# Gate/up of a SwiGLU block: Strassen products added onto read PSUM regions, the element-wise work on VectorE, weight splits in product order

## The chip, the cores and the metric

The kernel runs on one core of a Trainium2 chip. The metric is the time of one execution on the device in microseconds, as the median of several runs; less is better. TensorE does the matrix products, VectorE, ScalarE and GpSimd the element-wise work, and SyncE issues most of the transfers. SBUF is the memory on the core from which the engines work, and PSUM is the memory into which TensorE adds its products; a PSUM bank holds 512 fp32 numbers for each of 128 partitions.

## The reference

A hybrid decoder trunk of two layers on 512 tokens with 1024 channels, in fp32. Each layer is a mixer (layer 0: a forgetting attention beside a sparse attention; layer 1: trailing means over 2, 4, 8 and 16 positions) and then a SwiGLU block, both between RMS norms. The change concerns the first half of the SwiGLU blocks:

```python
DEPTH, SEQ, D_MODEL, FFN_HIDDEN = 2, 512, 1024, 2816
h = rmsnorm(x, g2)
act = silu(h @ w_gate) * (h @ w_up)      # "gate/up": (512, 1024) x (1024, 2816), twice
x = x + rmsnorm(act @ w_down, g3)        # "down"
```

## The kernel before

Every fp32 product is made of three fast ones: each operand is split into a high part (a copy rounded to the fast format, on ScalarE, L237) and a low part (the rest, a subtraction, L238), and `three` (L326 to L328) adds high x high, low x high and high x low in PSUM. Tiles named `wh` and `wl` are the parts of a weight block, `uh`/`ul` and `th`/`tl` those of the input.

The class `Ffn` computes gate/up. The 2816 columns are 22 chunks of 128, taken as 11 pairs. For a pair and one of the two weights (an *item*; gate and up alternate, 22 items a layer) the 256 columns by 1024 rows of the weight are a 2 x 2 matrix of blocks, a11, a12, a21, a22 (first index the column chunk, second the half of the rows), and so is the input (halves of rows, halves of the tokens). A Strassen-Winograd step makes the four 128 x 256 quadrants of the result from seven block products (named after their weight side: 11, 12, 22, s1, s2, s3, s4) instead of eight, each of 12 matmuls of 128x256. The s are sums of the a blocks, made by `comb` in place on the raw tiles (L906); the sums on the input's side come from `combine` (tiles `tt`, L873), once a layer. For the first three pairs of layer 0 and the first two of layer 1 (`self.ws`) two products with the first half of the tokens ran ahead in `front` while the norm of the second half was computed; their items have five products instead of seven. I call them *short*, the others *long*. `run` takes a long pair, a short pair, and so on, and then the long pairs that are left.

An item's two raw tiles (`wr`, 512 KB each) are loaded by SyncE (L894); the tag has four buffers, so the tiles of item i+2 take those of item i. The parts have ten buffers, five products' worth. `run` writes the splits of item i+1 (`pair_weights`), then the first products of item i (`begin`), the last of item i-1 (`end`, then `gate_done` or `up_done`), and the rest of item i (`middle`). Engines work in the order that the program is written in, apart from priorities; `comb` has a raised one. The products lie in three PSUM banks (psA, psS, psO), one half bank each; p5 and p7, p4 and p6 share a bank. VectorE adds them up in tiles `comb` by seven sums of 128x256 (L951 to L957 and L963, the last of an item). `next_engine` deals operations out in turn by a string: 'vg' means VectorE and GpSimd alternately. `sadd` (weight and input sums) is 'vg', `mul` (the gate-up product, L977) 'g', the low parts 'v'. After the last item, `down` multiplies the result by the third weight (L774 to L776).

Of the kernel before, what the change touches and what calls it, by code (L numbers as in the profile page):

```python
# [13 lines left out]
P = 128  # L14
# [39 lines left out]
    sadd='vg',  # L54
    mul='g',
# [57 lines left out]
def trunk(ctx: ExitStack, tc, x, norm_g, w_in, b_f, cmp_pe, cmp_w1, cmp_w2, w_out,  # L113
# [186 lines left out]
    def transpose_pair(dst, srcs, ks, tag, gcol=None):  # L300
        """dst(k) -> (hi, lo) of [128, 256]: the transposed column blocks ks of two token tiles"""
# [36 lines left out]
    # ================= layer 0: FoX || NSA =================  # L338
# [30 lines left out]
    # -- block compression --  # L369
# [63 lines left out]
    # -- keys and queries, stacked along the contraction --  # L433
# [49 lines left out]
    # -- values: [token, d] with high and low parts side by side --  # L483
# [36 lines left out]
    # -- forget gates and branch gates, projected beside the values of the NSA branches --  # L520
# [30 lines left out]
    # -- softmax and P^T for one (head, branch) and half of the queries --  # L551
# [215 lines left out]
    # -- out[token, :] = sum over contraction chunks; the last chunks token tile by token tile --  # L767
# [60 lines left out]
    class Ffn:  # L828
# [8 lines left out]
        def weights(self, p):  # L837
            """the first column chunk of a pair, whose two products with the first half of the tokens run ahead"""
            self.ws[p] = [load_w(cols(w_[self.layer], 2 * p * P, P), [P, KC, P], pair_g if p < CFG["eg"] else None)
                          for w_ in (w_gate, w_up)]  # L840
# [23 lines left out]
        def combine(self):  # L864
            """T1 = B12 - B11, T2 = B22 - T1, T3 = B22 - B12, T4 = B21 - T2, each transposed and split"""
# [23 lines left out]
        def pair_weights(self, w_, p):  # L889
            """the blocks of two column chunks and the sums of a Strassen-Winograd step, high and low parts"""  # L890
# [16 lines left out]

            if p not in self.ws:
                put("11", a11)
            put("22", a22)  # L910
            comb(a22, a21, a22, ALU.add)
            put("s1", a22)
            comb(a21, a11, a21, ALU.subtract)
            put("s3", a21)
            if p not in self.ws:
                put("12", a12)
            comb(a11, a22, a11, ALU.subtract)
            put("s2", a11)
            comb(a12, a12, a11, ALU.subtract)
            put("s4", a12)  # L920
            return W

        def run(self):
# [6 lines left out]
            def prod(o, w, b):  # L930
                for k in range(4):
                    three(o, w[0][k], w[1][k], b[0][k], b[1][k], k == 0, k == 3)

            def begin(W, p, i):
                m = {"pre": self.acts[2 * p + i] if p in self.ws else None, "W": W, "a": BANK("psA"), "b": BANK("psS"), "c": BANK("psO"), "x": XE([P, 4, 256], label="comb")}
                m["p1"], m["p5"], m["p7"], m["p4"], m["p6"] = (
                    m["a"][:, 0:256], m["b"][:, 0:256], m["b"][:, 256:512], m["c"][:, 0:256], m["c"][:, 256:512])
                if m["pre"] is None:
                    prod(m["p1"], W["11"], B11)
                    nc.scalar.activation(m["x"][:, 0, :], m["p1"], AF.Copy)  # L940
                prod(m["p4"], W["22"], T[4])
                return m

            def middle(m):
                W, x_ = m["W"], m["x"]
                prod(m["p5"], W["s1"], T[1])
                prod(m["p7"], W["s3"], T[3])
                if m["pre"] is None:
                    prod(m["p1"], W["12"], B21)
                prod(m["p6"], W["s2"], T[2])  # L950
                nc.vector.tensor_add(x_[:, 1, :], m["p6"], x_[:, 0, :] if m["pre"] is None else m["pre"][:, 256:])  # L951
                nc.vector.tensor_add(x_[:, 2, :], m["p7"], x_[:, 1, :])
                nc.vector.tensor_add(x_[:, 3, :], m["p5"], x_[:, 2, :])
                nc.vector.tensor_add(x_[:, 1, :], m["p5"], x_[:, 1, :])
                nc.vector.tensor_add(x_[:, 2, :], m["p4"], x_[:, 2, :])
                if m["pre"] is None:
                    nc.vector.tensor_add(x_[:, 0, :], m["p1"], x_[:, 0, :])  # L957

            def end(m, last):
                x_ = m["x"]  # L960
                p3 = BANK("psS")[:, 0:256] if last else m["p5"]
                prod(p3, m["W"]["s4"], B22)
                nc.vector.tensor_add(x_[:, 1, :], p3, x_[:, 1, :])  # L963

            def gate_done(m):
                x_ = m["x"] if m["pre"] is None else m["x"][:, 1:, :]
                nc.scalar.activation(x_, x_, AF.Silu)

            def up_done(p, g, m):
# [3 lines left out]
                for r in range(2):  # L973
                    r0 = 2 * r if r or m["pre"] is None else 1
                    a_ = self.acts[2 * p + r].rearrange("p (a b) -> p a b", a=2)[:, r0 - 2 * r:, :]
                    rows = slice(r0, 2 * r + 2)
                    next_engine("mul").tensor_tensor(a_, xg[:, rows, :], xu[:, rows, :], op=ALU.mult)  # L977

            def finish_(i):
                end(ms[i], i == len(todo) - 1)  # L980
# [5 lines left out]
            ws = [self.pair_weights(todo[0][1], todo[0][0])]  # L986
            ms = []
            for i in range(len(todo)):
                if i + 1 < len(todo):
                    ws.append(self.pair_weights(todo[i + 1][1], todo[i + 1][0]))  # L990
# [195 lines left out]
```

## Time and profile before

| quantity | value |
|---|---|
| time, median of 3 runs | 1079.62 us (1078.86 to 1079.63) |
| profiled execution, span | 1076.4 us |
| its gate/up, first combine sum to last item's end, layer 0 | 304.69 to 548.07 us |
| the same, layer 1 | 711.60 to 950.49 us |
| TensorE busy | 1032.2 us, 96% |
| VectorE busy | 783.5 us, 73% |
| ScalarE busy | 563.5 us, 52% |
| GpSimd busy | 511.0 us, 47% |

The profiled execution is told by its span, from the first to the last instruction; no time of its own outside the span is recorded, and the median of the runs is 3.2 us longer than it. Busy times of engines overlap. A share over the whole span is an average over stages with different limits, so the rows further down are mostly cut at the ends of items.

### The profile page before, as it was taken

To read this page: it belongs to the slowest core of one execution; us is meant where nothing else is said; L and a number is where in the kernel's file an instruction comes from. 1 tells how busy PE (TensorE), PEld (TensorE's weight loads), DVE (VectorE), ACT (ScalarE), POOL (GpSimd) and SP (SyncE) were. 2 spreads that over 40 slices of the span, in tenths; PEclk is the share of its full clock that TensorE was granted. 3 is DMA by queue.
4 is the path that set the end of the run, shared out by engine and by line. 5 is a ranking of instruction groups with operands and counts; after the bars stand their busy time and mean duration, and the time that the engine had idled before them with its cause. 6 is when DMAs were issued, how large, how long until landed. Compare 5 with 4: busy or idle time off the path is not lost.

```text
span 1076.4 us, 18708 instructions
## 1 busy us (share of the span) xinstructions
PE 1032.2 (96%) x6892; PEld 944.7 (88%) x6892; DVE 783.5 (73%) x1488; ACT 563.5 (52%) x1172; POOL 511.0 (47%) x421
## 2 busy tenths in 40 slices
PE   7999999999999999999999998989999999999997
PEld 6899888977899989899988886989889999988886
DVE  4449797767578999999991034788999999992123
ACT  5557797688465344444472234664444444472221
POOL 3815667666762444434454353362444334454340
PEclk9999999999999999999999999799999999999999
DMA  7920202233603333333334355003343343334222
GB/s 226 205 62 21 79 12 70 61 115 121 177 22 97 112 107 109 105 113 98 104 113 132 118 159 154 21 11 90 97 118 101 96 118 99 99 118 137 88 69 79
DMA packets 153419, 108.55 MB, mean 101 GB/s; under 512 B 11764, under 2 KB 134512, under 8 KB 153328
## 3 DMA queue, kind: packets, MB, share of 16 engines
q1 hardware_dynamic: 152528, 106.22, 33.7%
q8 instruction: 54, 0.88, 0.3%
q10 hardware_dynamic: 800, 1.15, 0.3%
q14 instruction: 37, 0.30, 0.1%
HBM read 101.88 MB, written 2.10 MB: 97 GB/s over the span
## 4 chain that ended last, share of the span: by engine, by line
PE 73%; DVE 15%; ACT 4%; issue 4%; DMA 2%; POOL 2%; DVEq 0%; POOLq 0%; ACTq 0%; SPq 0%
PE psA L328 5%; PE psA L326 5%; PE psA L327 5%; DVE wl L238 5%; PE psS L326 5%; PE psS L328 5%; PE psS L327 5%; PE psO L326 3%; PE psO L327 3%; PE psO L328 3%; PE psT L774 2%; PE psT L775 2%; PE psO L775 2%; PE psT L776 2%; PE psO L774 2%
## 5 line engine op out<-in xcount | busy, mean ns | idle before, releaser
L237 ACT ACTIVATE wh<-wr 128x512 fp32r<-128x512 f32 x420 | 252.8, 626 | 314.2 <-DVE wr L906 106.9
L238 DVE TENSOR_TENSOR wl<-wr,wh 128x512 fp32r<-128x512 f32 x318 | 297.0, 959 | 106.0 <-ACT wh L237 105.3
L238 POOL TENSOR_TENSOR wl<-wr,wh 128x512 fp32r<-128x512 f32 x102 | 144.4, 1426 | 137.7 <-ACT wh L237 128.6
L328 PE MATMUL psA<-uh,wl 128*128 128x256 f32 (+1 forms) x408 | 129.3, 317 | 0.5 <-DVE wl L238 0.5
L326 PE MATMUL psA<-uh,wh 128*128 128x256 f32 (+1 forms) x408 | 128.7, 315 | 0.4 <-ACT comb L940 0.4
L327 PE MATMUL psA<-ul,wh 128*128 128x256 f32 (+1 forms) x408 | 128.1, 314 | 0.0
L906 POOL TENSOR_TENSOR wr<-wr,wr 128x512 f32<-128x512 f32 x44 | 57.4, 1304 | 142.0 <-DVE wr L906 97.6
L906 POOL TENSOR_TENSOR wr<-wr 128x512 f32<-128x512 f32 x44 | 59.3, 1348 | 105.9 <-DVE wl L238 80.1
L326 PE MATMUL psS<-th,wh 128*128 128x256 f32 x352 | 100.9, 287 | 6.6 <-ACT wh L237 4.8
L328 PE MATMUL psS<-th,wl 128*128 128x256 f32 x352 | 101.4, 288 | 4.5 <-DVE wl L238 4.3
L327 PE MATMUL psS<-tl,wh 128*128 128x256 f32 x352 | 100.5, 286 | 0.0
L328 PE MATMUL psO<-th,wl 128*128 128x256 f32 x352 | 99.8, 284 | 0.6 <-DVE wl L238 0.6
L327 PE MATMUL psO<-tl,wh 128*128 128x256 f32 x352 | 99.8, 284 | 0.0
L326 PE MATMUL psO<-th,wh 128*128 128x256 f32 x352 | 99.5, 284 | 0.0
L328 PEld LDWEIGHTS psA<-uh,wl 128*128 128x128 f32 x408 | 78.3, 192 | 6.9 <-DVE wl L238 2.8
L326 PEld LDWEIGHTS psA<-uh,wh 128*128 128x128 f32 x408 | 78.2, 192 | 4.6 <-ACT comb L940 0.6
L327 PEld LDWEIGHTS psA<-ul,wh 128*128 128x128 f32 x408 | 78.3, 192 | 3.8
L977 POOL TENSOR_TENSOR act<-comb,comb 128x512 f32<-128x512 f32 (+1 forms) x44 | 71.9, 1649 | 11.6 <-DVE comb L963 6.2
L326 PEld LDWEIGHTS psS<-th,wh 128*128 128x128 f32 x352 | 67.7, 192 | 8.0 <-ACT wh L237 5.8
L328 PEld LDWEIGHTS psS<-th,wl 128*128 128x128 f32 x352 | 67.8, 193 | 6.8 <-DVE wl L238 6.7
L264 POOL TENSOR_SCALAR E<-E,ri 128x128 f32<-128x128 f32 (+3 forms) x48 | 54.6, 1139 | 40.0 <-DVE ri L582 16.7
L328 PEld LDWEIGHTS psO<-th,wl 128*128 128x128 f32 x352 | 67.4, 192 | 1.5 <-DVE wl L238 1.5
(343 smaller groups left out, 2972.2 us busy)
## 6 DMA issues: line engine op xcount, KB each, us to landing
wr<-in_ffn_w_gate_dram SPq DMA_DIRECT2D x49, 512.0 KB
wr<-in_ffn_w_up_dram SPq DMA_DIRECT2D x49, 512.0 KB
wr<-in_ffn_w_down_dram SPq DMA_DIRECT2D x44, 512.0 KB
wr<-in_attn_w_in_dram SPq DMA_DIRECT2D x20, 512.0 KB
wr<-in_attn_w_out_dram SPq DMA_DIRECT2D x8, 512.0 KB
x<-in_x_dram SPq DMA_DIRECT2D x4, 512.0 KB
gbc<-in_norm_g_dram SPq DMA_DIRECT2D x8, 256.0 KB
h<-in_x_dram SPq DMA_DIRECT2D x4, 512.0 KB
```

The lines of the kernel that those rows point to most:

```text
L237: nc.scalar.activation(hi, src, AF.Copy)
L238: next_engine(key).tensor_tensor(lo, src, r32(hi), op=ALU.subtract)
L264: (nc.vector if k == "v" else nc.gpsimd).tensor_scalar(e, e, s1, None, op0=ALU.mult)
L326: nc.tensor.matmul(psum, wh, ah, start=first, stop=False)
L327: nc.tensor.matmul(psum, wh, al, start=False, stop=False)
L328: nc.tensor.matmul(psum, wl, ah, start=False, stop=last)
L774: nc.tensor.matmul(o, acts[c][0][:, tok], wh[k], start=first, stop=False)
L775: nc.tensor.matmul(o, acts[c][0][:, tok], wl[k], start=False, stop=False)
L776: nc.tensor.matmul(o, acts[c][1][:, tok], wh[k], start=False, stop=last)
L906: next_engine("sadd").tensor_tensor(o, x0, x1, op=op)
L977: next_engine("mul").tensor_tensor(a_, xg[:, rows, :], xu[:, rows, :], op=ALU.mult)
```

## The change

GpSimd's part of gate/up goes to VectorE: `sadd` and `mul` become 'v'. Two products get no PSUM region of their own any more: 22 is added by TensorE onto the region of p7 after VectorE read that, and s4 onto p5. In long items 12 is added onto p1 likewise, after ScalarE read it. A fourth block tile, s3, replaces one of the sums in place. The seven sums of 128x256 in an item become three (L956 to L958) and one of 128x512 that adds one `comb` row to both halves of a bank (L966). The bank psO is not used in gate/up any more. Quadrant p1 is read from PSUM by the silu (L972) and by the product (L979) in long pairs. The gate-up product is L979 to L981, and the combinations stand in L907 (these are line numbers of the changed kernel). `pair_weights` becomes a generator that gives the splits in the order in which the products are done: 11 and s2 of item i+1, then 22 and s4 of item i, then s3, s1 and 12 of item i+1. The products go 11, s2 of an item, then 22, s4 of the item before, then s3, s1, 12.

```diff
-    sadd='vg',
-    mul='g',
+    sadd='v',
+    mul='v',
...
         def pair_weights(self, w_, p):
             raws = []
             for a in range(2):
                 raw = T([P, KC, P], "wr", CFG["wr"])
@@ -905,20 +906,23 @@
                 with tc.high_priority(CFG["hpw"]):
                     next_engine("sadd").tensor_tensor(o, x0, x1, op=op)
 
+            s3 = JK("s3").rearrange("p (k c) -> p k c", k=4)
             if p not in self.ws:
                 put("11", a11)
-            put("22", a22)
-            comb(a22, a21, a22, ALU.add)
-            put("s1", a22)
-            comb(a21, a11, a21, ALU.subtract)
-            put("s3", a21)
+            comb(s3, a11, a21, ALU.subtract)
+            comb(a21, a21, a22, ALU.add)
+            comb(a11, a21, a11, ALU.subtract)
+            put("s2", a11)
+            yield W
+            put("s3", s3)
+            put("s1", a21)
             if p not in self.ws:
                 put("12", a12)
-            comb(a11, a22, a11, ALU.subtract)
-            put("s2", a11)
             comb(a12, a12, a11, ALU.subtract)
+            yield W
+            put("22", a22)
             put("s4", a12)
-            return W
+            yield W
 
         def run(self):
             rest = [p for p in range(NF // 2) if p not in self.ws]
@@ -927,67 +931,72 @@
             B11, B21, B22 = self.block(0, 0), self.block(1, 0), self.block(1, 1)
             T = self.T
 
-            def prod(o, w, b):
+            def prod(o, w, b, start):
+
                 for k in range(4):
-                    three(o, w[0][k], w[1][k], b[0][k], b[1][k], k == 0, k == 3)
+                    wh, wl, bh, bl = w[0][k], w[1][k], b[0][k], b[1][k]
+                    nc.tensor.matmul(o, wh, bh, start=start and k == 0, stop=False, skip_group_check=True)
+                    nc.tensor.matmul(o, wh, bl, start=False, stop=False, skip_group_check=True)
+                    nc.tensor.matmul(o, wl, bh, start=False, stop=k == 3, skip_group_check=True)
 
             def begin(W, p, i):
-                m = {"pre": self.acts[2 * p + i] if p in self.ws else None, "W": W, "a": BANK("psA"), "b": BANK("psS"), "c": BANK("psO"), "x": XE([P, 4, 256], label="comb")}
-                m["p1"], m["p5"], m["p7"], m["p4"], m["p6"] = (
-                    m["a"][:, 0:256], m["b"][:, 0:256], m["b"][:, 256:512], m["c"][:, 0:256], m["c"][:, 256:512])
-                if m["pre"] is None:
-                    prod(m["p1"], W["11"], B11)
+                pre = self.acts[2 * p + i] if p in self.ws else None
+                m = {"pre": pre, "W": W, "a": BANK("psA"), "c": BANK("psS"), "x": XE([P, 4, 256], label="comb")}
+                m["p1"], m["p6"], m["p5"], m["p7"] = m["a"][:, 0:256], m["a"][:, 256:], m["c"][:, 0:256], m["c"][:, 256:]
+                if pre is None:
+                    prod(m["p1"], W["11"], B11, True)
                     nc.scalar.activation(m["x"][:, 0, :], m["p1"], AF.Copy)
-                prod(m["p4"], W["22"], T[4])
+                prod(m["p6"], W["s2"], T[2], pre is not None)
                 return m
 
             def middle(m):
                 W, x_ = m["W"], m["x"]
-                prod(m["p5"], W["s1"], T[1])
-                prod(m["p7"], W["s3"], T[3])
+                prod(m["p7"], W["s3"], T[3], True)
+                prod(m["p5"], W["s1"], T[1], False)
+                nc.vector.tensor_add(x_[:, 0, :], m["p6"], x_[:, 0, :] if m["pre"] is None else m["pre"][:, 256:])
+                nc.vector.tensor_add(x_[:, 3, :], m["p7"], x_[:, 0, :])
+                nc.vector.tensor_add(x_[:, 3, :], m["p5"], x_[:, 3, :])
                 if m["pre"] is None:
-                    prod(m["p1"], W["12"], B21)
-                prod(m["p6"], W["s2"], T[2])
-                nc.vector.tensor_add(x_[:, 1, :], m["p6"], x_[:, 0, :] if m["pre"] is None else m["pre"][:, 256:])
-                nc.vector.tensor_add(x_[:, 2, :], m["p7"], x_[:, 1, :])
-                nc.vector.tensor_add(x_[:, 3, :], m["p5"], x_[:, 2, :])
-                nc.vector.tensor_add(x_[:, 1, :], m["p5"], x_[:, 1, :])
-                nc.vector.tensor_add(x_[:, 2, :], m["p4"], x_[:, 2, :])
+                    prod(m["p1"], W["12"], B21, False)
+
+            def end(m):
+                x_ = m["x"]
+                prod(m["p7"], m["W"]["22"], T[4], False)
+                prod(m["p5"], m["W"]["s4"], B22, False)
+                nc.vector.tensor_tensor(x_[:, 1:3, :], m["c"].rearrange("p (a b) -> p a b", a=2),
+                                        x_[:, 0:1, :].to_broadcast([P, 2, 256]), op=ALU.add)
+
+            def gate_done(m):
+                x_ = m["x"]
                 if m["pre"] is None:
-                    nc.vector.tensor_add(x_[:, 0, :], m["p1"], x_[:, 0, :])
-
-            def end(m, last):
-                x_ = m["x"]
-                p3 = BANK("psS")[:, 0:256] if last else m["p5"]
-                prod(p3, m["W"]["s4"], B22)
-                nc.vector.tensor_add(x_[:, 1, :], p3, x_[:, 1, :])
-
-            def gate_done(m):
-                x_ = m["x"] if m["pre"] is None else m["x"][:, 1:, :]
-                nc.scalar.activation(x_, x_, AF.Silu)
+                    nc.scalar.activation(x_[:, 0, :], m["p1"], AF.Silu)
+                nc.scalar.activation(x_[:, 1:, :], x_[:, 1:, :], AF.Silu)
 
             def up_done(p, g, m):
                 xg, xu = g["x"], m["x"]
                 if m["pre"] is None:
                     self.acts[2 * p], self.acts[2 * p + 1] = RAW(2 * p), RAW(2 * p + 1)
-                for r in range(2):
-                    r0 = 2 * r if r or m["pre"] is None else 1
-                    a_ = self.acts[2 * p + r].rearrange("p (a b) -> p a b", a=2)[:, r0 - 2 * r:, :]
-                    rows = slice(r0, 2 * r + 2)
-                    next_engine("mul").tensor_tensor(a_, xg[:, rows, :], xu[:, rows, :], op=ALU.mult)
+                    nc.vector.tensor_mul(self.acts[2 * p][:, 0:256], m["p1"], xg[:, 0, :])
+                next_engine("mul").tensor_tensor(self.acts[2 * p][:, 256:], xg[:, 1, :], xu[:, 1, :], op=ALU.mult)
+                next_engine("mul").tensor_tensor(self.acts[2 * p + 1].rearrange("p (a b) -> p a b", a=2), xg[:, 2:, :], xu[:, 2:, :], op=ALU.mult)
 
             def finish_(i):
-                end(ms[i], i == len(todo) - 1)
+                end(ms[i])
                 if i % 2 == 0:
                     gate_done(ms[i])
                 else:
                     up_done(todo[i][0], ms[i - 1], ms[i])
 
-            ws = [self.pair_weights(todo[0][1], todo[0][0])]
+            gens = [self.pair_weights(w_, p) for p, w_ in todo]
+            ws = [next(gens[0])]
+            next(gens[0])
             ms = []
             for i in range(len(todo)):
                 if i + 1 < len(todo):
-                    ws.append(self.pair_weights(todo[i + 1][1], todo[i + 1][0]))
+                    ws.append(next(gens[i + 1]))
+                next(gens[i])
+                if i + 1 < len(todo):
+                    next(gens[i + 1])
                 ms.append(begin(ws[i], todo[i][0], i % 2))
                 if i:
                     finish_(i - 1)
```

Two places show what that does to the order on VectorE. `comb_9` to `comb_11` are the results of three successive items, 9 and 10 a long pair; `wl` are low parts, `wr` raw tiles (54 and 55 of item 9, 56 and 57 of item 10, 58 and 59 of item 11). At the border of items 9 and 10, VectorE had before:

```order
L238 TENSOR_TENSOR wl_112_5281<-wr_56_5276,wh_112_5280 128x512
L238 TENSOR_TENSOR wl_113_5285<-wr_57_5278,wh_113_5284 128x512
L951 TENSOR_TENSOR comb_9_5315<-psO_45_5314,comb_9_5315 128x256
L906 TENSOR_TENSOR wr_57_5278<-wr_57_5278 128x512
L952 TENSOR_TENSOR comb_9_5315<-psS_96_5313,comb_9_5315 128x256
L957 TENSOR_TENSOR comb_9_5315<-psA_38_5312,comb_9_5315 128x256
L953 TENSOR_TENSOR comb_9_5315<-psS_96_5313,comb_9_5315 128x256
L954 TENSOR_TENSOR comb_9_5315<-psS_96_5313,comb_9_5315 128x256
L238 TENSOR_TENSOR wl_114_5290<-wr_57_5278,wh_114_5289 128x512
L955 TENSOR_TENSOR comb_9_5315<-psO_45_5314,comb_9_5315 128x256
L906 TENSOR_TENSOR wr_56_5276<-wr_57_5278,wr_56_5276 128x512
L238 TENSOR_TENSOR wl_115_5295<-wr_57_5278,wh_115_5294 128x512
```

There it has now:

```order
L958 TENSOR_TENSOR comb_9_5280<-psS_96_5279,comb_9_5280 128x256
L238 TENSOR_TENSOR wl_111_5254<-wr_56_5241,wh_111_5253 128x512
L238 TENSOR_TENSOR wl_112_5258<-wr_55_5138,wh_112_5257 128x512
L238 TENSOR_TENSOR wl_113_5262<-wr_54_5136,wh_113_5261 128x512
L238 TENSOR_TENSOR wl_114_5266<-s3_10_5245,wh_114_5265 128x512
L956 TENSOR_TENSOR comb_10_5403<-psA_39_5401,comb_10_5403 128x256
L238 TENSOR_TENSOR wl_115_5270<-wr_57_5243,wh_115_5269 128x512
L238 TENSOR_TENSOR wl_116_5274<-wr_56_5241,wh_116_5273 128x512
L907 TENSOR_TENSOR wr_56_5241<-wr_56_5241 128x512
L966 TENSOR_TENSOR comb_9_5280<-psS_96_5279,comb_9_5280 128x512
L907 TENSOR_TENSOR s3_11_5376<-wr_58_5372,wr_59_5374 128x512
L907 TENSOR_TENSOR wr_59_5374<-wr_59_5374 128x512
```

Before, the low parts of item 10 (from `wr_56`, `wr_57`) began ahead of item 9's sums, and those of item 9 were all done. Now the low parts of 22 and s4 of item 9 (`wl_112` from `wr_55`, `wl_113` from `wr_54`, the last reads of these tiles) stand behind the low part of s2 of item 10 (`wl_111`), and s3 of item 11, the first read of `wr_58` and `wr_59`, stands seven rows further down.

The second place is the border between items 7 and 8, a short gate and a short up item (`wr_52` and `wr_53` are item 8's). Before, on VectorE:

```order
L238 TENSOR_TENSOR wl_99_4967<-wr_50_4942,wh_99_4966 128x512
L238 TENSOR_TENSOR wl_100_5072<-wr_53_5069,wh_100_5071 128x512
L906 TENSOR_TENSOR wr_53_5069<-wr_53_5069 128x512
L951 TENSOR_TENSOR comb_7_5098<-psO_43_5097,act_3_4078 128x256
L952 TENSOR_TENSOR comb_7_5098<-psS_94_5096,comb_7_5098 128x256
L238 TENSOR_TENSOR wl_101_5077<-wr_53_5069,wh_101_5076 128x512
L953 TENSOR_TENSOR comb_7_5098<-psS_94_5096,comb_7_5098 128x256
L954 TENSOR_TENSOR comb_7_5098<-psS_94_5096,comb_7_5098 128x256
L906 TENSOR_TENSOR wr_52_5067<-wr_53_5069,wr_52_5067 128x512
L955 TENSOR_TENSOR comb_7_5098<-psO_43_5097,comb_7_5098 128x256
L238 TENSOR_TENSOR wl_102_5082<-wr_53_5069,wh_102_5081 128x512
L238 TENSOR_TENSOR wl_103_5087<-wr_52_5067,wh_103_5086 128x512
```

And now:

```order
L980 TENSOR_TENSOR act_9_5104<-comb_5_4820,comb_6_4943 128x256
L981 TENSOR_TENSOR act_10_5105<-comb_5_4820,comb_6_4943 128x512
L907 TENSOR_TENSOR s3_8_5039<-wr_52_5035,wr_53_5037 128x512
L957 TENSOR_TENSOR comb_7_5066<-psS_94_5065,comb_7_5066 128x256
L907 TENSOR_TENSOR wr_53_5037<-wr_53_5037 128x512
L958 TENSOR_TENSOR comb_7_5066<-psS_94_5065,comb_7_5066 128x256
L907 TENSOR_TENSOR wr_52_5035<-wr_53_5037,wr_52_5035 128x512
L907 TENSOR_TENSOR wr_52_5035<-wr_52_5035 128x512
L238 TENSOR_TENSOR wl_98_5044<-wr_52_5035,wh_98_5043 128x512
L238 TENSOR_TENSOR wl_99_5048<-wr_51_4914,wh_99_5047 128x512
L238 TENSOR_TENSOR wl_100_5052<-wr_50_4912,wh_100_5051 128x512
L238 TENSOR_TENSOR wl_101_5056<-s3_8_5039,wh_101_5055 128x512
```

Before, the first low part of item 8 (`wl_100`, of 22) stood ahead of item 7's sums. Now the first one (`wl_98`, of s2) stands behind the sums of item 7 (L957, which reads p7, and L958, which reads p5) and behind four combinations of item 8's raw tiles.

## Rows read from the trace of the kernel before

**Rows 1.** The page: engine totals, and the granted clock in 40 slices.

```profile
PE 1032.2 (96%) x6892; PEld 944.7 (88%) x6892; DVE 783.5 (73%) x1488; ACT 563.5 (52%) x1172; POOL 511.0 (47%) x421
...
PEclk9999999999999999999999999799999999999999
```

**Rows 2.** Timeline of TensorE's matmuls, 440 to 482 us: start, duration, instruction.

```profile
445.06 0.28 PE L326 MATMUL psS<-uh,wh 128*128 128x256 f32 x1
...
445.90 0.28 PE L327 MATMUL psS<-ul,wh 128*128 128x256 f32 x1
```

**Rows 3.** Timeline of VectorE: the last sum of two items, same columns.

```profile
478.81 0.41 DVE L963 TENSOR_TENSOR comb<-psS,comb 128x256 f32<-128x256 f32 x1
...
540.72 0.41 DVE L963 TENSOR_TENSOR comb<-psS,comb 128x256 f32<-128x256 f32 x1
```

**Rows 4.** Windows between item ends: length; PE, PEld, DVE, ACT, POOL busy; clock; DMA; GB/s.

```profile
304.69:347.05 42.36, 40.64 (x339) 40.00 (x338) 36.59 (x58) 25.18 (x49) 20.98 (x17) 1.00 0.26 75
...
370.92:410.34 39.42, 37.30 (x291) 36.36 (x290) 36.71 (x59) 16.72 (x28) 16.79 (x12) 0.96 0.37 108
410.34:448.86 38.52, 36.36 (x291) 35.05 (x290) 36.79 (x60) 16.70 (x28) 16.79 (x12) 1.00 0.38 110
448.86:548.07 99.21, 98.08 (x800) 96.27 (x799) 94.36 (x156) 48.99 (x85) 42.80 (x31) 1.00 0.37 109
...
770.52:809.94 39.42, 37.31 (x291) 36.37 (x290) 36.70 (x60) 16.73 (x28) 16.78 (x12) 0.96 0.37 107
809.94:950.49 140.55, 139.42 (x1136) 136.85 (x1135) 134.80 (x220) 68.69 (x119) 60.88 (x43) 1.00 0.37 108
```

**Rows 5.** Timeline of VectorE inside one item, 454 to 459 us.

```profile
454.06 0.41 DVE L952 TENSOR_TENSOR comb<-psS,comb 128x256 f32<-128x256 f32 x1
454.39 0.41 DVE L957 TENSOR_TENSOR comb<-psA,comb 128x256 f32<-128x256 f32 x1
...
456.98 1.28 DVE L238 TENSOR_TENSOR wl<-wr,wh 128x512 fp32r<-128x512 f32 x2
458.18 0.42 DVE L963 TENSOR_TENSOR comb<-psS,comb 128x256 f32<-128x256 f32 x1
458.51 1.67 DVE L238 TENSOR_TENSOR wl<-wr,wh 128x512 fp32r<-128x512 f32 x1
```

**Rows 6.** Timeline of GpSimd at the same place.

```profile
458.34 1.30 POOL L906 TENSOR_TENSOR wr<-wr 128x512 f32<-128x512 f32 x1 [2.77 <-DVE wl L238]
```

**Rows 7.** Timeline of VectorE near 304 us, a 512-column operation on PSUM.

```profile
303.98 0.68 DVE L814 TENSOR_TENSOR mq<-psO,gbc 128x512 f32<-128x512 f32 x1
```

**Rows 8.** Timeline of SyncE's queue: issues of raw weight tiles.

```profile
361.20 1.90 SPq L894 DMA_DIRECT2D wr<-in_ffn_w_up_dram  x2
...
457.68 3.74 SPq L894 DMA_DIRECT2D wr<-in_ffn_w_up_dram  x2
```

**Rows 9.** Windows of half a microsecond behind those issues, columns as in rows 4.

```profile
362.00:362.50 0.50, 0.50 (x6) 0.50 (x6) 0.50 (x2) 0.35 (x1) 0.00 (x0) 1.00 0.31 58
...
367.00:367.50 0.50, 0.50 (x6) 0.50 (x6) 0.50 (x1) 0.26 (x1) 0.21 (x1) 1.00 0.10 30
...
458.50:459.00 0.50, 0.50 (x7) 0.50 (x6) 0.50 (x2) 0.37 (x1) 0.50 (x1) 1.00 0.20 57
...
459.50:460.00 0.50, 0.50 (x6) 0.50 (x6) 0.50 (x1) 0.50 (x2) 0.14 (x1) 1.00 0.98 294
...
460.50:461.00 0.50, 0.50 (x6) 0.50 (x5) 0.50 (x2) 0.50 (x2) 0.00 (x0) 1.00 0.40 118
```

**Rows 10.** Windows of one microsecond at a short pair, columns as in rows 4.

```profile
395.00:396.00 1.00, 0.50 (x2) 0.30 (x2) 1.00 (x2) 0.28 (x2) 0.96 (x1) 1.00 0.00 0
...
397.00:398.00 1.00, 1.00 (x9) 1.00 (x8) 1.00 (x3) 0.05 (x1) 0.14 (x1) 0.74 0.00 0
...
399.00:400.00 1.00, 1.00 (x6) 1.00 (x6) 1.00 (x2) 0.63 (x1) 0.14 (x1) 0.50 0.00 0
```

**Rows 11.** Timeline of TensorE: the first matmul of the down projection, layer 0.

```profile
547.84 0.50 PE L774 MATMUL psT<-wh,ah 128*128 128x512 f32 x1 [1.12 <-ACT ah L211]
```

## The prediction

> **What bounds the kernel now.** I read the engine totals first, then the windows cut at the ends of the gate/up items, then the timelines of VectorE and TensorE inside them.
>
> TensorE is busy for 96% of the span and its clock is reduced in one slice of 40 only; VectorE stands at 73%, GpSimd at 47% [rows 1]. So the kernel is close to TensorE's own time, and the change can give at most what TensorE loses inside gate/up. To size that: matmuls follow each other every 0.12 us (445.06 to 445.90 is seven steps) [rows 2]. A long pair (14 products, 168 matmuls) therefore takes at least 168 x 0.12 = 20.16 us and a short pair (10 products, 120) 14.4 us. The last VectorE add of a gate item comes at 478.81 and, three long pairs later, at 540.72: 20.64 us each [rows 3]. A long pair loses 0.48 us. A long and a short pair together need 34.56 us, and took 39.42, 38.52 and 39.42 [rows 4]: some 4 to 5 us are lost in each. The reader should see two regimes: long pairs at TensorE's rate, short pairs well off it.
>
> VectorE is what TensorE waits for. In 448.86 to 548.07 it is busy 94.36 of 99.21 us [rows 4], but not by its own work alone. Where nothing runs on GpSimd, the next instruction starts 0.60 us after a 128x512 operation out of SBUF (two from 456.98, the next at 458.18) and 0.33 us after a 128x256 sum with a PSUM operand (454.06 to 454.39) [rows 5]. A long pair has 14 low-part subtractions, 4 weight combinations and 14 such sums on it: 18 x 0.60 + 14 x 0.33 = 15.5 us of 20.64. The rest is contention: the subtraction at 458.51 takes 1.67 us [rows 5] while GpSimd runs the combination of 458.34 [rows 6].
>
> **The change part by part.** (a) *Combinations and gate-up product from GpSimd to VectorE.* Per long pair, four more 128x512 operations (4 x 0.60 = 2.4 us) and products of 256 + 256 + 512 columns (0.33 + 0.33 + 0.60 = 1.27). GpSimd falls silent in gate/up, and the stretching of VectorE with it.
>
> (b) *Sums on TensorE.* The 14 sums become 6 of 128x256 (2.0) and two of 128x512. No row shows a two-half PSUM sum with a broadcast operand; below it costs what the SBUF operation does, 0.60, above what the 128x512 PSUM multiplication lasts, 0.68 [rows 7]. I take 0.60; the difference is 0.16 us a pair. TensorE's products do not become fewer: accumulating onto a read region adds no matmul. Long pair on VectorE afterwards: 22 x 0.60 + 2.0 + 1.2 + 1.27 = 17.7 us, below TensorE's 20.16. Short pair: 12.4 before (14 x 0.60 + 12 x 0.33), 14.9 after, just above TensorE's 14.4.
>
> (c) *Long pairs.* With cover of 2.5 us per pair, I expect TensorE's own rate, 20.16 (at worst 20.64, nothing gained). Behind the short pairs stand five long pairs in layer 0 and seven in layer 1 [rows 4]: **12 x -0.47 = -5.6 us**, bounds 0 and -7.4. (The latter is what these two stretches lose in all: 99.21 - 800 x 0.12 and 140.55 - 1136 x 0.12, 3.2 + 4.2.)
>
> (d) *Splits in product order: the raw tiles come free later.* The order on VectorE shows it. The two raw tiles of item i+2 are loaded into those of item i, which are free after the low parts of 22 and s4 of item i. These stood before s3 and s4 of the next item; now they stand behind s2 of item i+1. And s3 of item i+2, the first thing that reads the new tiles, stands ahead of a21, a11, two sums, s2(i+2), 22(i+1) and s4(i+1) on an engine that works in order. So one turn "s4(i), load, s3(i+2), ..., s4(i+1)" now takes one item; before, the load had two.
>
> Its price: a lone 512 KB load issued at 457.68 [rows 8] moves data from 458.5 to about 460.9 [rows 9], 3.2 us. Two loads, issued from 361.20 to 363.10 [rows 8], move data from 362.0 to some 367.3 [rows 9], which is 4.2 us behind the last issue. Here two loads would be issued 0.6 us apart, as the two low parts end. With 0.8 us to the first data and twice 1.8 us for 512 KB at the 294 GB/s of a full window [rows 9], the second lands 4.4 us after the first's issue, 3.8 after s4's low part; bounds are 3.2 (as if alone) and 5.0 (the pair's slower rate), and I take 4.2, as in the measured pair. Behind it: three combinations (1.8), two sums (0.67), three low parts (1.8), and the wait for ScalarE's high part, which no row shows alone here: an estimate of 0.8 to 1.1, one operation of ScalarE (563.5 us in 1172 of them is 0.48 [rows 1]) and about as much for the hand-overs. That makes 5.0 to 5.4. **The loop is 9.2 to 9.6 us per item**: below a long item's 10.08, above a short item's 7.2.
>
> The Trainium skill bears on this in "DMA: Bandwidth & Descriptors", section "Anatomy of one DMA — SWDGE (gpsimd) path": a load costs about 2.0 us and its bytes over 436 GB/s. That is 3.2 us for 512 KB, and the trace agrees with its 3.2, although the page fits another path than SyncE's queue. For the two loads it would give 4.4 us from the first issue, an estimate, so a loop of about 9.0 and a total some 4 us below mine.
>
> (e) *Short pairs.* In a cycle the two short items go at the loop's 9.2 to 9.6 (18.4 to 19.2) and the long pair at 20.16: 38.6 to 39.4, against 38.5 to 39.4 now. At the border from a short gate to a short up item the low part of s2(8) stands behind the sum that waits for p5 of item 7, with two combinations and a high part between; TensorE has nothing left for some 2 us there, which the loop's slack swallows. **0**, bounds -1.5 and +1.5 for each of five cycles.
>
> (f) *Layer starts.* With the durations above, and counted in the order of its instructions, VectorE has 29.8 us of work from the first combine operation to the first item's end now, and 36.7 after, in a stretch of 42.36 in which it is busy 36.59 with GpSimd beside it for 20.98 [rows 4]. The extra 6.9 replaces about as much stretching: **0**, bounds -3 and +3 a layer.
>
> (g) *Hand-over to the down projection.* The last product is followed by a 512 sum, and products of 256 and 512 columns, 0.60 + 0.33 + 0.60, where there was one sum of 0.33 and GpSimd's product; TensorE already waits 1.12 us for the split activations there [rows 11]. The down weights' tiles come free one item later too. **+1 a layer, +2**, bounds 0 and +3.
>
> Sum: -5.6 + 0 + 0 + 2 = -3.6. The profiled execution has a span of 1076.4 us; the median of the runs is 1079.62, 3.2 outside the span, and I leave those as they are: **1079.6 - 3.6 = 1076.0 us**.
>
> **Rivals.** About 0.2% (2.2 us) is what a measurement of this kernel can tell from no change.
>
> *R1, the short pairs gain too* (0.14): GpSimd's stretching makes today's 4 to 5 us per cycle, and the load loop is nearer 8 us. For it: VectorE is at 36.71 of 39.42 in the cycle with GpSimd busy for 16.79 [rows 4]. Against: the combinations and two loads in one turn hardly fit into 8 us. A cycle of 16.0 + 20.16 = 36.2 gives -3 for each of five: 1061.
>
> *R2, slower by the load loop* (0.20): if the second load lands 5.0 us or more after s4's low part, or a hand-over adds as much, the turn is 10.3 us. It decides from 10.08, where it passes TensorE's long item; long pairs then stay at 20.6, and short pairs go from 18.8 (39.42 - 20.64) to 20.6: 5 x 1.8 + 2 = +11, 1091. For it: two loads at a time were not back to back in any row, and the measured pair lasted long; against: the DMA share is 0.37 in these windows [rows 4], so little else is in the way.
>
> *R3, the clock* (0.10): before, TensorE did two to four matmuls a microsecond from 394 to 397 and then ran at 0.50 of its 2.4 GHz, at 1.2, until 400.6 [rows 10]: about 1.6 us lost. Every short item begins with s2, so the border of (e) stands ahead of both short items of a pair. If each empties TensorE so, there are ten drops where the windows with a clock of 0.96 [rows 4] show two now: 8 x 1.6 = +12.8 on my sum, 1089.
>
> *R4, no change* (0.22): the long pairs' 0.48 us is not VectorE's, or is given back at the starts and hand-overs: 1079.6.
>
> **How the numbers follow.** The forecast, with its own range of 1071 to 1077.5, has 0.34. Faster is the forecast and R1: 0.48. Same is R4: 0.22. Slower are R2 and R3: 0.30. The range must reach to R1 and to R2: 1060 to 1091 leaves out the outer half of each, 0.07 and 0.10.
>
> **What would show it.** Right: in the profile after, GpSimd has no row in gate/up; VectorE's low parts last 0.68 alone and none 1.67; item ends of a long pair lie 20.2 us apart; SyncE's pairs of gate/up loads lie 0.6 us apart and s3 waits for a DMA in short items. Wrong: long pairs at 20.6 with TensorE waiting for a high or low part (R4 or R2), short pairs under 17 us (R1), or granted clocks of 0.5 in every short pair (R3).

## The result and the profile after

The changed kernel takes 1132.13 us (median of 4 runs, 1131.04 to 1132.92) against 1079.62: the ratio is 1.0491, with a 95% interval of 1.0477 to 1.0506. It is slower by 52.5 us where the forecast was 3.6 faster.

Cut at the ends of the items of gate/up (the starts of L963 before and L966 after), both spans divide so:

| stretch (us) | before | after | difference |
|---|---|---|---|
| start to the first item's end, layer 0 | 347.05 | 350.21 | +3.2 |
| first to last item's end, layer 0 | 201.02 | 225.05 | +24.0 |
| to the first item's end, layer 1 | 198.59 | 202.71 | +4.1 |
| first to last item's end, layer 1 | 203.83 | 225.46 | +21.6 |
| to the end | 125.91 | 127.37 | +1.5 |

So 45.6 of 54.4 us lie inside gate/up. The engine totals and the granted clock by slices, from the page of the changed kernel:

```profile
PE 1050.4 (93%) x6892; PEld 956.8 (85%) x6892; DVE 760.9 (67%) x1528; ACT 559.5 (49%) x1189; POOL 314.1 (28%) x276
...
PEclk9999999999999999999999998889999999999999
```

Against [rows 1], TensorE is busy 93% instead of 96%, GpSimd fell from 511.0 to 314.1 us, and VectorE is busy *less*, 760.9 instead of 783.5: it lost its stretching, and yet the kernel is slower. An engine that became the bound would have shown more. The windows between item ends (length; PE, PEld, DVE, ACT, POOL busy; clock; DMA share; GB/s):

```profile
398.15:413.23 15.08, 10.88 (x76) 10.47 (x75) 10.48 (x18) 3.35 (x6) 0.00 (x0) 0.89 0.36 97
413.23:457.40 44.17, 37.91 (x291) 36.53 (x290) 34.50 (x62) 15.80 (x29) 0.00 (x0) 0.96 0.35 96
501.14:568.05 66.91, 62.62 (x504) 60.80 (x503) 55.81 (x101) 28.88 (x54) 0.00 (x0) 1.00 0.33 94
```

The first is one short gate item, 15.08 us long, in which TensorE is busy for 10.88. The second holds the work of one cycle, a short up item, a long pair and the next short gate item, and lasts 44.17 us; a cycle took 39.42 or 38.52 in [rows 4]. The third is three long pairs, 66.91 us. Its ends on VectorE's timeline answer to [rows 3]:

```profile
501.14 0.68 DVE L966 TENSOR_TENSOR comb<-psS,comb 128x512 f32<-128x512 f32 x1
...
568.05 0.69 DVE L966 TENSOR_TENSOR comb<-psS,comb 128x512 f32<-128x512 f32 x1
```

A long pair takes 22.30 us instead of 20.64, with VectorE busy for 55.81 of 66.91 and GpSimd for nothing. TensorE, VectorE and the transfers (DMA share 0.33) all have time to spare, which is what a loop of waits looks like. The chain that ended last shows it, over one turn (start, duration, piece):

```profile
518.98 3.94 DMA wr<-in_ffn_w_gate_dram
523.03 0.64 ACT wh L237
523.69 0.69 DVE wl L238
524.39 0.60 DVE comb L966
524.99 0.61 DVE s L907
525.62 0.69 DVE wr L907
526.31 0.34 DVE comb L957
526.65 0.61 DVE wr L907
527.36 0.64 ACT wh L237
528.03 1.30 DVE wl L238 x2
529.35 4.03 DMA wr<-in_ffn_w_up_dram
```

From the issue of a load to the issue of the next, 10.37 us, everything is in a line: the first raw tile lands (3.94), its high and low part for product 11, the sum L966 that stands next on VectorE, s3, a21, a sum, a11, the high part for s2, and the low parts of s2 and 22, the second of which frees a tile of the item before, and the next load is issued. TensorE is nowhere in it. The turn before lasted 518.98 - 506.83 = 12.15 us, and there s3 waited for the second tile. SyncE's queue, two rows of VectorE (s3 and a11) and windows in between:

```profile
506.83 0.99 SPq L895 DMA_DIRECT2D wr<-in_ffn_w_up_dram  x2
```

```profile
513.72 0.69 DVE L907 TENSOR_TENSOR s<-wr,wr 128x512 f32<-128x512 f32 x1 [0.85 <-DMA wr<-in_ffn_w_up_dram]
...
516.20 0.68 DVE L907 TENSOR_TENSOR wr<-wr,wr 128x512 f32<-128x512 f32 x1
```

```profile
511.00:511.50 0.50, 0.50 (x6) 0.50 (x5) 0.00 (x0) 0.50 (x1) 0.00 (x0) 1.00 1.07 279
...
512.50:513.00 0.50, 0.50 (x7) 0.50 (x6) 0.37 (x1) 0.00 (x0) 0.00 (x0) 1.00 0.07 17
513.00:513.50 0.50, 0.50 (x6) 0.50 (x6) 0.00 (x0) 0.00 (x0) 0.00 (x0) 1.00 0.02 6
...
513.20:513.50 0.30, 0.30 (x5) 0.30 (x4) 0.00 (x0) 0.00 (x0) 0.00 (x0) 1.00 0.00 0
```

The reader of the second tile starts 6.9 us after the first issue. In this turn the chain that ended last runs along TensorE instead:

```profile
516.84 0.13 PE psA L940
517.00 0.64 ACT wh L237
```

The high part of s2 needs a11, done at 516.88 (516.20 + 0.68), and it also waits for a product that ends at 516.97. The two come within 0.1 us, so the load's line took as long as TensorE's. Between the first and the last item's end the chain passes through a load of raw tiles in most turns; where it does not, it runs mostly along TensorE, from 484 to 517, from 821 to 831 and from 847 to 860 us.

### The profile page after: what moved, and what is told of

It reads as the page before. It is cut to its first block, busy times and chain, and to the rows that moved or that the text cites. A ratio compares the mean times of both kernels' runs of the same rounds, so it can differ in the third digit from the quotient of the medians.

```text
span 1130.8 us, 18514 instructions
## 1 busy us (share of the span) xinstructions
PE 1050.4 (93%) x6892; PEld 956.8 (85%) x6892; DVE 760.9 (67%) x1528; ACT 559.5 (49%) x1189; POOL 314.1 (28%) x276
## 4 chain that ended last, share of the span: by engine, by line
PE 44%; DVE 23%; DMA 18%; ACT 7%; issue 4%; POOL 2%; SPq 0%; ACTq 0%; DVEq 0%; POOLq 0%
DMA wr<-in_ffn_w_gate_dram 9%; DVE wl L238 7%; DMA wr<-in_ffn_w_up_dram 7%; DVE wr L907 4%; ACT wh L237 4%; PE psT L776 2%; PE psO L776 2%; PE psT L774 2%; PE psO L774 2%; PE psT L775 2%; PE psO L775 2%; PE psS L938 2%; PE psS L940 2%; DVE s L907 2%; PE psO L627 2%
## 5 line engine op out<-in xcount | busy, mean ns | idle before, releaser
L238 DVE TENSOR_TENSOR wl<-wr,wh 128x512 fp32r<-128x512 f32 x274 | 190.8, 717 | 151.8 <-ACT wh L237 149.0
L938 PE MATMUL psS<-th,wh 128*128 128x256 f32 x528 | 155.6, 295 | 17.0 <-ACT wh L237 10.5
L939 PEld LDWEIGHTS psS<-tl,wh 128*128 128x128 f32 x528 | 104.4, 198 | 0.0
L938 PE MATMUL psA<-uh,wh 128*128 128x256 f32 x272 | 78.2, 287 | 2.0 <-ACT wh L237 2.0
L940 PE MATMUL psA<-uh,wl 128*128 128x256 f32 x272 | 77.8, 286 | 0.2 <-DVE wl L238 0.2
L939 PE MATMUL psA<-ul,wh 128*128 128x256 f32 x272 | 77.5, 285 | 0.0
L938 PE MATMUL psA<-th,wh 128*128 128x256 f32 x176 | 53.5, 306 | 21.3 <-ACT wh L237 16.6
L907 DVE TENSOR_TENSOR wr<-wr 128x512 f32<-128x512 f32 x88 | 60.4, 689 | 1.8
L576 ACT ACTIVATE E<-E,mn 128x128 f32<-128x128 f32 (+1 forms) x96 | 53.5, 558 | 8.3 <-DVE mn L574 7.6
L938 PEld LDWEIGHTS psA<-th,wh 128*128 128x128 f32 x176 | 35.3, 201 | 24.7 <-ACT wh L237 18.2
L940 PE MATMUL psA<-th,wl 128*128 128x256 f32 x176 | 52.9, 301 | 0.8 <-DVE wl L238 0.7
## 6 DMA issues: line engine op xcount, KB each, us to landing
wr<-in_ffn_w_gate_dram SPq DMA_DIRECT2D x49, 512.0 KB
wr<-in_ffn_w_up_dram SPq DMA_DIRECT2D x49, 512.0 KB
wr<-in_ffn_w_down_dram SPq DMA_DIRECT2D x44, 512.0 KB
wr<-in_attn_w_in_dram SPq DMA_DIRECT2D x20, 512.0 KB
wr<-in_attn_w_out_dram SPq DMA_DIRECT2D x8, 512.0 KB
x<-in_x_dram SPq DMA_DIRECT2D x4, 512.0 KB
h<-in_x_dram SPq DMA_DIRECT2D x4, 512.0 KB
```

What stands on the lines that cost most here:

```text
L238: next_engine(key).tensor_tensor(lo, src, r32(hi), op=ALU.subtract)
L576: nc.scalar.activation(e, e, AF.Exp, bias=mn[:, n_:n_ + 1], scale=-1.0, accum_out=sm[:, n_:n_ + 1])
L907: next_engine("sadd").tensor_tensor(o, x0, x1, op=op)
L938: nc.tensor.matmul(o, wh, bh, start=start and k == 0, stop=False, skip_group_check=True)
L939: nc.tensor.matmul(o, wh, bl, start=False, stop=False, skip_group_check=True)
L940: nc.tensor.matmul(o, wl, bh, start=False, stop=k == 3, skip_group_check=True)
```

## The experiments

Theory A says that this turn sets the pace. Theory B says that VectorE's longer work and its order do. C says that most of the loss is TensorE's clock.

**e1: splits in item order.**

```diff
+                next(gens[i])
                 if i + 1 < len(todo):
                     ws.append(next(gens[i + 1]))
-                next(gens[i])
-                if i + 1 < len(todo):
                     next(gens[i + 1])
```

> The changed kernel, but the low parts of 22 and s4 of an item are written ahead of those of 11 and s2 of the next, not behind. Theory A (the turn 's4 split, load of two raw tiles, s3 two items on, s4 split of the next item' sets the pace of every item): the tiles come free about one item's first splits earlier and the load has an item's time again, so long pairs fall from 23 us to 20.2 to 20.7 and the time to 1066 to 1082 us. Theory B (VectorE's own longer work and its order around the sums set the pace, the loads only show where it waits): the same work stands on VectorE, so 1120 us or more. Theory C (TensorE's clock falls in the gaps and that is most of the loss): as B, unless the gaps go.

1108.94 us, ratio 1.0286 (1.0271 to 1.0301). 23 us came back, and both theories missed: the stretches between item ends are 213.3 us in both layers, not 201. The groups of waits from 330 to 570 us (total, times, longest) of this kernel, and then of the changed one:

```profile
ACT wh L237 <- PE psS L939: 34.8, 30, 3.7
ACT wh L237 <- PE psA L939: 26.7, 17, 3.9
```

```profile
ACT wh L237 <- PE psA L939: 9.3, 7, 2.6
...
ACT wh L237 <- PE psS L939: 7.4, 9, 2.3
```

ScalarE now waits for products to be done: perhaps since the ten buffers of parts are handed round in the order of the splits, which no longer is that of the products. That was not tried by itself, and e10 below leaves it at most 11 of the 30 us that e1 stands above the kernel before.

**e2: raw tiles by halves of the rows.**

```diff
-                raw = T([P, KC, P], "wr", CFG["wr"])
-                nc.sync.dma_start(raw, cols(w_, (2 * p + a) * P, P))
+                raw = T([P, 4, 2 * P], "wr", CFG["wr"])
+                nc.sync.dma_start(raw, cols(w_, 2 * p * P, 2 * P, 4 * a, 4))
...
-            (a11, a12), (a21, a22) = ((r_[:, 0:4, :], r_[:, 4:8, :]) for r_ in raws)
+            (a11, a21), (a12, a22) = ((r_[:, :, 0:P], r_[:, :, P:]) for r_ in raws)
```

> The changed kernel with its split order, but a raw tile holds the same row half of both column chunks: one tile a11 and a21, the other a12 and a22, so that the first is free an item earlier and only one load of 512 KB is left in the turn. Same bytes, same memory, same operations. Theory A: the turn falls from about 11 us to about 8, below TensorE's 10.08 for a long item; long pairs at 20.2 to 20.7, time 1062 to 1085 us. Theory B: 1115 us or more.

1094.44 us, ratio 1.0148 (1.0131 to 1.0166): 37.7 us back, with the same work on VectorE. Between item ends gate/up takes 412.6 us instead of 450.5. One thing beside the turn changed: a half tile is read in runs of 1024 bytes instead of 512. A lone load's data were in after 3.1 to 3.2 us in five of six such loads of e2 and e12, and after 3.2 to 3.6 us in nearly all of the kernel before. That is little beside the 1.6 us by which long pairs got shorter, and e6 below keeps the old form. Theory A holds for the larger part, but the span stays 14.9 us over that of the kernel before, 7.7 between item ends and 7.2 at the starts and after gate/up. They are not in the long pairs (10.27 + 10.40 us in two successive items). At the border of the short gate and the short up item TensorE's timeline still shows:

```profile
395.85 0.38 PE L938 MATMUL psA<-th,wh 128*128 128x256 f32 x1 [2.35 <-ACT wh L237]
397.19 0.58 PE L940 MATMUL psA<-th,wl 128*128 128x256 f32 x1 [0.83 <-DVE wl L238]
```

**e3 and e4: the engines alone.** e3 is the changed kernel with `sadd='vg'`, `mul='g'`; e4 is the kernel before with `sadd='v'`, `mul='v'`.

> The changed kernel with sadd back to VectorE and GpSimd alternately and mul back to GpSimd; its order of splits stays. Theory A: two of the combinations in the turn last 1.3 us or more on GpSimd instead of 0.6 and stretch VectorE's beside them, so the turn gets longer: 1135 to 1165 us. Theory B: VectorE is relieved of 17.7 - 14 us a pair: 1095 to 1120 us.

> The kernel before with sadd and mul on VectorE and nothing else changed. VectorE then has 22 x 0.60 + 14 x 0.33 + 1.27 = 19.1 us a long pair, without stretching, TensorE 20.16. Theory A: the load keeps two items' time, so no new loop: 1066 to 1084 us. Theory B: VectorE's work on the path makes it slower: 1095 us or more.

e3: 1168.42 us, ratio 1.0844 (1.0824 to 1.0863), beyond A's upper end; a long pair takes 13.24 + 10.88 = 24.12 us. That fits a turn lengthened by slower combinations, but e3 moves the product too. e4: 1086.68, ratio 1.0078 (1.0063 to 1.0093), between the two: no loop, but no gain either. Its short pairs got faster (a cycle of 38.6 us), its long ones slower, 11.03 + 10.50 = 21.53 us.

**e5 and e6: a fifth raw tile.** Both have `xe=3` instead of 4 for the room; e6 has `wr=5`.

> The changed kernel with three instead of four buffers of the tag xe (4 KB a partition), the control for the next run. Both theories: within some 10 us of the changed kernel's 1132, with long pairs near 22 us.

> As the control, with the 4 KB given to a fifth raw tile; split order, tile shape and loads stay. Theory A (turn of split and load): one of an item's two tiles is free an item earlier, so the turn holds one load of 512 KB instead of two; gate/up of the two layers together 20 to 40 us shorter than in the control. Theory B (VectorE's own order): less than 8 us.

1136.12 and 1097.81 us (two runs each; ratios to the kernel before 1.0534, 1.0513 to 1.0555, and 1.0179, 1.0159 to 1.0199). Gate/up, both layers between item ends, went from 443.5 to 417.6 us, 25.9 less, as A expected: only when a tile comes free was changed. A further 11.6 us fell between the layers, outside the question.

**e7: half tiles, `mul='g'`.**

> The half tiles of e2 with the gate-up product back on GpSimd, three operations a pair. If the residue of e2 over the kernel before (1094 against 1079) is VectorE's longer work, it falls: 1080 to 1090. If it is the second loop (high parts that wait for a free split buffer) it stays: 1092 to 1100.

1093.21, ratio 1.0130 (1.0113 to 1.0147), the same as e2 within the noise. The product's engine is not the residue.

**e8 and e9: the kernel before, one of the two moved.** e8 has `sadd='v'`, e9 `mul='v'`.

> The kernel before with the combinations on VectorE alone; the product stays on GpSimd. In e4 long pairs took 21.5 us with both moved, with 19.1 us of work on VectorE. If the product behind the silu is what makes VectorE wait there: 20.2 to 20.7 a pair and 1066 to 1080. If the combinations do: 21.3 or more, 1080 to 1088.

> The kernel before with the gate-up product on VectorE; the combinations stay on both engines. e8 put the combinations alone on VectorE and long pairs took 21.4 us instead of 20.6. If it is the combinations in VectorE's line that cost, long pairs stay at 20.2 to 20.7 here and the time at 1073 to 1081. If any more work on VectorE costs: 21.0 or more a pair, 1083 to 1090.

e8: 1086.34, ratio 1.0074 (1.0055 to 1.0092), long pairs of 10.26 + 11.15 = 21.41 us. e9: **1068.79 us, ratio 0.9904 (0.9890 to 0.9919)**, faster than both kernels and than I expected. A long pair of e9, one window:

```profile
505.21:525.38 20.17, 20.17 (x170) 20.17 (x169) 19.02 (x36) 9.80 (x17) 5.18 (x4) 1.00 0.36 106
```

20.17 us, TensorE busy throughout, VectorE for 19.02. And what e8's TensorE waits for, then VectorE's timeline at the same place of the next item:

```profile
479.23 0.39 PE L326 MATMUL psS<-uh,wh 128*128 128x256 f32 x1 [0.58 <-DVE comb L954]
```

```profile
486.48 0.42 DVE L951 TENSOR_TENSOR comb<-psO,comb 128x256 f32<-128x256 f32 x1 [0.38 <-PE psO L328]
486.82 0.68 DVE L906 TENSOR_TENSOR wr<-wr 128x512 f32<-128x512 f32 x1
...
488.08 0.68 DVE L906 TENSOR_TENSOR wr<-wr,wr 128x512 f32<-128x512 f32 x1
488.68 0.42 DVE L953 TENSOR_TENSOR comb<-psS,comb 128x256 f32<-128x256 f32 x1
489.01 0.42 DVE L954 TENSOR_TENSOR comb<-psS,comb 128x256 f32<-128x256 f32 x1
```

In this order the product s4 overwrites p5, so it must wait until L954 has read p5, and on one engine two combinations stand among the sums ahead of L954. In e8 the combinations cost by where they stand, not by their sum: over the pair from 489.01 us the steps of TensorE's matmuls over 0.12 us add up to 1.3 us, 1.0 of it where it waits for L954 and the rest at a low part. In e4, with both moved, L954 is the smaller share (0.7 us in 80, where low parts cost 0.9), so what costs there is not settled.

**e10 and e11: half tiles with the item order of e1; half tiles with `sadd='vg'`, `mul='g'`.**

> Half tiles as in e2 and the item order of e1 together. If e1 kept its loss because s3 still waited for both tiles, the half tiles take that away: 1080 to 1092. If e1 lost by high parts that wait for a split buffer whose product comes later than the order of the splits, that stays: 1098 to 1110, above e2's 1094.

> Half tiles with combinations on both engines and the product on GpSimd, as the kernel before has them. If the combinations stand in the turn behind the one load that is left, GpSimd's 1.3 us for each lengthens it: 1105 to 1130. If VectorE's line is what costs in e2, it is relieved: 1075 to 1090.

e10: 1090.36, ratio 1.0098 (1.0079 to 1.0117), somewhat below e2, so the wait for both tiles was part of e1's loss. e11: 1105.92, ratio 1.0241 (1.0218 to 1.0263), some 12 us over e7, from which it differs in the combinations alone. That is the slower range, but not for the reason given: its long pairs take 11.72 + 8.71 = 20.43 us, no longer than e7's. The loss lies in the short pairs and at the starts. That the first product of a short item there waits for slower combinations is likely, but was not tried.

**e12: half tiles, s3 first in short items.**

```diff
             comb(s3, a11, a21, ALU.subtract)
+            if p in self.ws:
+                put("s3", s3)
...
-                prod(m["p6"], W["s2"], T[2], pre is not None)
+                if pre is None:
+                    prod(m["p6"], W["s2"], T[2], False)
+                else:
+                    prod(m["p7"], W["s3"], T[3], True)
```

(s2 takes the place that s3 leaves, in the splits and in `middle`.)

> Half tiles as in e2, and in short items s3 (one combination away from the raw tiles) is split and multiplied first instead of s2 (three combinations away); long items as they are. If the border of the items of short pairs, where TensorE waits for s2 and then loses its clock, is what e2 has left over the kernel before, each of ten short items gets its first product one to two combinations earlier and fewer drops of the clock follow: 1080 to 1089. If the residue is elsewhere (starts, hand-overs, long pairs): 1091 to 1097.

1078.34, ratio 0.9994 (0.9980 to 1.0008): 16 us back, and level with the kernel before. Between item ends gate/up takes 195.92 and 200.12 us, 8.8 less than before; the layer starts and what follows gate/up take back as much (350.42 to the first end, 202.20 between, 127.64 at the end; 8.7 more).

## Why the prediction was wrong

**The mechanism was named; its size and its chance were wrong.** Rival R2 said that the load's turn decides from 10.08 us, and the forecast put it at 9.2 to 9.6. Step (d) failed in one term, the time from the first issue to s3. I took 4.8 us for it (0.6 + 4.2). Where s3 waited for the second tile, it was 5.7 to 7.2, as here:

```profile
383.87 1.00 SPq L895 DMA_DIRECT2D wr<-in_ffn_w_gate_dram  x2
```

```profile
389.70 0.69 DVE L907 TENSOR_TENSOR s<-wr,wr 128x512 f32<-128x512 f32 x1 [1.29 <-DMA wr<-in_ffn_w_gate_dram]
```

I had read the load off the windows up to the end of its data, but the reader starts some 0.5 us later (513.2 to 513.72 above). Where s3 did not wait for the second tile, it still started some 6.0 us after the issue (518.98 to 524.99): I left out that the split of 11 (0.64 + 0.69) stands ahead of s3 and waits for the first tile itself, and that L966 (0.60) stands there too. What stands behind s3 was sized right: 5.0 to 5.4 in the forecast, 4.4 and 5.3 in the two turns above. Together the turn was 10.4 to 12.2 us from 361 us on in layer 0. The Trainium skill's "DMA: Bandwidth & Descriptors", section "Anatomy of one DMA — SWDGE (gpsimd) path", would give 4.4 us for two such loads, an estimate; the measured 5.7 to 7.2 decide, and they come from another path than the page's.

R2's price, +11, was too low as well. It let long pairs stay at 20.6, and the three above took 22.30 each: the two stretches of long pairs behind the short ones, 99.21 and 140.55 us in [rows 4], took 108.74 and 149.18, 18.2 more. The stretches with short pairs grew by the other 27.4, where R2 had 9. e2 and e6 show the turn by two different ways of breaking it.

**Step (e) failed by its cover.** I had TensorE empty for 2 us at the border of the short items and the loop's slack to swallow it. The border, on VectorE, TensorE and in windows:

```profile
401.51 0.69 DVE L907 TENSOR_TENSOR s<-wr,wr 128x512 f32<-128x512 f32 x1 [1.61 <-DMA wr<-in_ffn_w_up_dram]
...
403.05 0.42 DVE L958 TENSOR_TENSOR comb<-psS,comb 128x256 f32<-128x256 f32 x1
403.39 0.68 DVE L907 TENSOR_TENSOR wr<-wr,wr 128x512 f32<-128x512 f32 x1
```

```profile
404.92 0.38 PE L938 MATMUL psA<-th,wh 128*128 128x256 f32 x1 [4.18 <-ACT wh L237]
```

```profile
402.00:403.00 1.00, 0.00 (x0) 0.00 (x0) 1.00 (x3) 0.00 (x0) 0.00 (x0) 1.00 0.00 0
...
406.00:407.00 1.00, 1.00 (x7) 1.00 (x6) 1.00 (x3) 0.96 (x2) 0.00 (x0) 0.50 0.00 0
```

s3 waits for the load until 401.51, L958 stands ahead of a11 (403.39), and only then come s2's high part and its product: TensorE idles 4.18 us, and then runs at 0.50, that is at 1.2 GHz, as in [rows 10]. A wait can't be absorbed by a loop whose turn runs through it. With the loop broken the border cost 16 us more than it does with s3 first (e2 against e12).

**R3 came with it.** Inside gate/up the granted clock was below 0.97 in 41 windows of one microsecond, before in 13; the shares missing in them add up to 17.1 and 5.1 us. The 12.0 more are near the 12.8 that R3 had, by luck: of the eight stretches of such windows (three before) only four stand in short pairs, two in the start of layer 1 and two in long pairs. They follow the gaps and are no cause of their own: e12, whose short items get their first product earlier, has 3.4, and none in its short pairs. Theory C has at most these 12 of the 52.5 us.

**Step (c) was right about what is there to gain, and (a) wrong about what takes it.** VectorE's low parts last 0.69 us on average in the three long pairs, and GpSimd does nothing there. But 2.5 us of cover a pair was a sum, and sums don't say what stands ahead of what. In e9 the pair takes 20.17, the forecast's 20.16; with the combinations on VectorE (e8, e4) it takes 21.4 to 21.5 in the old order.

**The small steps held.** (b) L966 lasts 0.68 us and the next instruction starts after 0.60 (524.39, 524.99 in the chain). (f) From the first combine operation to the first item's end the layers took 2.1 and 1.5 us more (305.79 to 350.21 against 42.36, 741.38 to 777.97 against 35.06), inside their bounds of 3 but not 0. (g) The first matmul of down begins 1.09 us behind the last sum's start at 575.26, where [rows 11] had it 0.23 ahead of that sum's: +1.3 for +1 (layer 1: +1.4).

```profile
576.35 0.50 PE L774 MATMUL psT<-wh,ah 128*128 128x512 f32 x1 [1.12 <-ACT ah L211]
```

R4 and R1 fell: the long pairs' 0.48 us can be had (e9), and the short pairs got slower.

## What to carry to other kernels

When splits or loads are reordered, write down for each buffer its last reader, the load that this releases, and everything that stands between that load's first reader and the next last reader on the engines that work in order; compare that turn with the bound engine's time, and count every instruction in the line. A buffer that holds things that are read at different times is free only after the last of them, so cut the load by time of use (e2: 38 us, a little of it perhaps from the transfers' longer runs). Free time on an engine is no cover for work that is put ahead of something another engine waits for: move one kind of work at a time, since here one half of the move was worth 10 us (e9) and the other cost 8 (e8).

## What the runs showed of the hardware

Of two loads of 512 KB that SyncE issued 0.6 to 0.7 us apart, the first one's reader started 3.9 to 4.4 us after the first issue in most pairs of gate/up (518.98 to 523.03) and up to 5.7 us after it in a few; the second one's reader, where it waited for nothing else, 5.7 to 7.2 us after it (506.83 to 513.72). A lone load's data were through after 3.2 us ([rows 8, 9]), but the end of the data is not yet the reader's start. In the windows above the transfers are nearly over at 512.0; a share of 0.07, about one of 16 engines, is left from 512.5 to 513.0, nothing is left after 513.2, and s3 starts at 513.72. So the last few packets and another half a microsecond hold up the whole tile. What these packets are was not tried.
